# Trunk of four token mixers on one core: branch D's projections moved to the front, three gate paths moved into the seven-product stage

## The chip, the cores and the metric

One Trainium2 chip, one of its cores. The metric is the device time of one execution in microseconds (us); the times shown are of three runs. The engines are named as the profile names them: PE is TensorE (matmuls; PEld is its weight load), DVE is VectorE, ACT is ScalarE, POOL is GpSimd, SP is SyncE, which here only issues DMAs.

## What is computed

One layer over x of 512 tokens by 2048 columns, in float32. One projection of x is cut into the inputs of four mixers, their gate paths and four merge gates:

```
h = jnp.einsum('bsd,de->bse', x, w_in[l])
(a_in, a_gate, u, v, b_gate, q, k, vv, c_gate,
 d_in, d_gate, g_logits) = jnp.split(h, SPLIT_POINTS, axis=-1)

y_a = pool_mixer(a_in, pool_w[l], pool_scale[l]) * jax.nn.silu(a_gate)
y_b = spatial_gating(u, v, sgu_ln_g[l], sgu_ln_b[l], sgu_w[l], sgu_b[l]) * jax.nn.silu(b_gate)
y_c = sliding_window_attention(q, k, vv, attn_sinks[l], band_bias) * jax.nn.silu(c_gate)
y_d = conformer_conv(d_in, conv_w[l], conv_b[l], conv_ln_g[l], conv_ln_b[l]) * jax.nn.silu(d_gate)
...
merged = gates[:, :, 0] * jnp.einsum('bsc,cd->bsd', branches[0], w_branch[l, 0])
...
out = jnp.einsum('bsd,de->bse', merged, w_out[l])
x = layer_norm(ALPHA * x + out, ln_g[l], ln_b[l])
```

A pools over trailing windows of 2, 4, 8 and 16 tokens and multiplies by a small matrix per group. B normalises v and mixes it over tokens in chunks of 128. C is attention in a window of 128. D forms val * sigmoid(gate), convolves it over 31 tokens per channel (31 taps), normalises and applies swish. The gate paths a_gate, b_gate and d_gate (ag, bg and dg in the kernel) have 1024 columns each.

## The kernel before

Every large product is made of three matmuls (`mm3`, L137 to L139): both operands are split into a high part (hi, an ACT copy, L113) and a low part (lo, a DVE subtraction, L114), and hi x hi, lo x hi and hi x lo are summed in PSUM. Weights come in blocks of 512 KB; a block that is brought in and split is one *task* of PE.

There are two ways to make a projection. In a *projection tile* (`proj`), 128 columns of the weights are the stationary operand and all 512 tokens move past: 2 tasks of 24 matmuls, and the result has channels on the partitions. In the *seven-product stage* (`quad`) a set of 1024 columns is computed with seven products of half-size blocks in place of eight: p1, p5, m6, p3, m7, p2, p4, each 4 tasks of 12 matmuls, 336 in all. The results have tokens on the partitions and go to DRAM through ACT's queue (`spill`). The sums of weight blocks that the products need are made in place: after a block's hi and lo are taken, POOL issues a DMA that adds the next block onto the raw one (L288, tables `ADDS`, `TAKES`), and the next product splits it again. Tag `ra` carries the chain p1, p5, m6 (then p4), `rc` the pair p3, m7, `rd` p2. The sums of x blocks are made at the start (`first`, `xcalc`, `xsplit`). DVE adds the products up (L350); ACT copies the first (L354).

`run` (L168) walks a plan of tasks. The bringing in and splitting of a block runs two tasks ahead of its use (`AHEAD`), through four raw buffers and three of hi and lo. Ahead of each task `drain` issues some entries of a queue of side work (`bg`), which holds the taps of D's convolution (`conv`, L588 and L591): 248 of 128x512 on DVE. The framework's scheduler then sets the order within each engine; each engine runs its order strictly in turn.

The order before: 9 sets (v for branch B, then 8 for the merge gates); `back` brings back a block of x that a sum overwrote; D's val and gate tiles (16), with the taps on DVE behind them, and v's normalisation (`v_norm`) between them; branch B with u and bg in turn; branch A, with ag tiles behind each group's product (`pool_mix`, `group_mm`); the 8 dg tiles; attention; merge and output.

Of the kernel before, what the change touches and what calls it, by code (L numbers as in the profile page):

```python
# [17 lines left out]
P = 128  # L18
S = 512
# [18 lines left out]
QUADS = 9  # L38
# [14 lines left out]
def kernel(  # L53
# [52 lines left out]
    def bank():  # L106
        return pools["psum"].tile([P, S], F32, name="ps", tag="ps")
# [60 lines left out]
    def run():  # L168
# [3 lines left out]
        for prep, f in plan:  # L172
# [3 lines left out]
            while nxt < len(todo) and len(ready) <= AHEAD:  # L176
                ready.append(todo[nxt]())
                nxt += 1
# [7 lines left out]

    def proj(name, j, mid=()):
        i = SLOT[name, j]
        for c in range(2):
            def f(hi, lo, c=c):  # L190
                if c == 0:
                    box[name, j] = bank()
                for k in range(8):
                    kt = c * 8 + k
                    s_ = slice(k * P, (k + 1) * P)
                    mm3(box[name, j].rearrange("p (a b) -> p a b", a=2), hi[:, s_], lo[:, s_],
                        xmov(xH, kt), xmov(xL, kt), kt == 0, kt == KT - 1)
# [15 lines left out]
    def leave():  # L213
        opened.pop().__exit__(None, None, None)
# [10 lines left out]
    gD = dram.tile([len(ORDER), NB, P, D], F32, name="gD")  # L225
    yD = dram.tile([len(ORDER), WT, P, S], F32, name="yD")
# [8 lines left out]
    def enter_q():  # L235
        pools["pairs"] = enter("pairs", bass.MemoryType.PSUM)
        p = pools["quad"] = enter("quad")
        q["H"] = p.tile([P, len(SUMS), HT, 2 * P], F32R, name="sH")
        q["L"] = p.tile([P, len(SUMS), HT, 2 * P], F32R, name="sL")
        for n, a in enumerate(("x11", "x12", "s1", "x22")):  # L240
            q[a] = (xH[:, n], xL[:, n])
# [3 lines left out]
    def spin():  # L245
        w = pair(0)
        for _ in range(9):
            T.matmul(w[:, 0, :P], lhsT=ones, rhs=ones, start=True, stop=True)

    def pair(n):  # L250
        return pools["pairs"].tile([P, 2, S], F32, name=f"pr{n}", tag=f"pr{n}", bufs=1)

    def wide(name):
        return pools["quad"].tile([P, 2, S], F32, name="o", tag="o", bufs=4)

    def load_x(n, to):
# [7 lines left out]
    def xsplit(n, name, h):  # L264
# [873 lines left out]
```

## Time and profile before

| | |
|---|---|
| median of 3 runs | 2128.75 us (2128.35 to 2130.6) |
| profiled execution, its time | 2129.99 us |
| its span, first to last instruction | 2128.3 us |
| mean granted clock | 0.995 |
| PE busy | 2097.0 us (99%) |
| DVE busy | 1211.0 us (57%) |
| ACT busy | 751.0 us (35%) |
| POOL busy | 183.5 us (9%) |

An instruction's record is longer than its share of the engine where instructions overlap: a matmul is recorded with 0.39 us, but they start 0.23 us apart. Paces are therefore read from starts. The granted clock is the share of TensorE's full clock that it was given in a stretch.

### The profile page before, as it was taken

To read this page: it belongs to the slowest core of one execution; us is meant where nothing else is said; L and a number is where in the kernel's file an instruction comes from. 1 tells how busy PE (TensorE), PEld (TensorE's weight loads), DVE (VectorE), ACT (ScalarE), POOL (GpSimd) and SP (SyncE) were. 2 spreads that over 40 slices of the span, in tenths; PEclk is the share of its full clock that TensorE was granted. 3 is DMA by queue.
4 is the path that set the end of the run, shared out by engine and by line. 5 is a ranking of instruction groups with operands and counts; after the bars stand their busy time and mean duration, and the time that the engine had idled before them with its cause. 6 is when DMAs were issued, how large, how long until landed. Compare 5 with 4: busy or idle time off the path is not lost.

```text
span 2128.3 us, 23836 instructions
## 1 busy us (share of the span) xinstructions
PE 2097.0 (99%) x9436; PEld 1739.4 (82%) x9436; DVE 1211.0 (57%) x1467; ACT 751.0 (35%) x912; POOL 183.5 (9%) x241
## 2 busy tenths in 40 slices
PE   7999999999999999999999999999999999999998
PEld 5788888888888788888888888888888888888886
DVE  6555555555555699996353432366674445444346
ACT  5344444444444332222242222255562222222220
POOL 2021112112112100000000000000000000000002
PEclk8999999999999999999999999999999999999999
DMA  9998899899889622343323333423334454435332
GB/s 249 259 213 214 234 210 221 228 222 211 227 232 179 228 91 98 99 159 109 111 93 104 109 129 124 154 89 99 99 134 164 160 179 166 168 129 204 102 119 80
DMA packets 103552, 340.52 MB, mean 160 GB/s; under 512 B 10677, under 2 KB 15829, under 8 KB 102672
## 3 DMA queue, kind: packets, MB, share of 16 engines
q1 hardware_dynamic: 63232, 208.06, 29.9%
q0 software_dynamic: 29840, 111.40, 23.7%
q10 hardware_dynamic: 10368, 19.53, 2.4%
q8 instruction: 74, 1.21, 0.2%
q14 instruction: 38, 0.31, 0.0%
HBM read 307.47 MB, written 34.63 MB: 161 GB/s over the span
## 4 chain that ended last, share of the span: by engine, by line
PE 95%; DMA 2%; issue 1%; DVE 1%; POOL 0%; SPq 0%; ACT 0%; POOLq 0%; DVEq 0%; ACTq 0%
PE ps L137 21%; PE ps L138 21%; PE ps L139 21%; PE pr L138 10%; PE pr L139 10%; PE pr L137 10%; DMA rd<-in_xt 1%; PE ps L874 1%; PE ps L858 1%; DMA o<-in_xt 1%; DMA rc<-in_wq 0%; PE ps L810 0%; PE ps L809 0%; PE ps L467 0%; PE ps L554 0%
## 5 line engine op out<-in xcount | busy, mean ns | idle before, releaser
L114 DVE TENSOR_TENSOR lo<-ra,hi 128x1024 fp32r<-128x1024 f32 x387 | 471.0, 1217 | 718.1 <-ACT hi L113 694.1
L113 ACT CAST hi<-ra 128x1024 fp32r<-128x1024 f32 x387 | 405.9, 1049 | 1059.6 <-PE ps L138 447.8
L137 PE MATMUL ps<-xH,hi 128*128 128x512 f32 x1184 | 463.9, 392 | 2.1 <-DVE o L350 2.1
L139 PE MATMUL ps<-xH,lo 128*128 128x512 f32 x1184 | 461.4, 390 | 0.0
L138 PE MATMUL ps<-xL,hi 128*128 128x512 f32 x1184 | 461.4, 390 | 0.0
L137 PEld LDWEIGHTS ps<-xH,hi 128*128 128x128 f32 x1184 | 222.7, 188 | 48.9 <-issue 3.7
L139 PEld LDWEIGHTS ps<-xH,lo 128*128 128x128 f32 x1184 | 222.6, 188 | 46.8
L138 PEld LDWEIGHTS ps<-xL,hi 128*128 128x128 f32 x1184 | 222.8, 188 | 45.6 <-issue 0.5
L137 PE MATMUL pr<-hi,xH 128*128 128x512 f32 x576 | 226.4, 393 | 7.3 <-ACT hi L113 5.0
L138 PE MATMUL pr<-lo,xH 128*128 128x512 f32 x576 | 226.8, 394 | 5.3 <-DVE lo L114 5.3
L139 PE MATMUL pr<-hi,xL 128*128 128x512 f32 x576 | 226.2, 393 | 1.6 <-DVE xL L114 1.6
L137 PE MATMUL ps<-hi,xH 128*128 128x512 f32 x472 | 183.7, 389 | 0.0
L139 PE MATMUL ps<-hi,xL 128*128 128x512 f32 x472 | 183.6, 389 | 0.0
L138 PE MATMUL ps<-lo,xH 128*128 128x512 f32 x472 | 183.6, 389 | 0.0
L138 PE MATMUL pr<-lo,sH 128*128 128x512 f32 x432 | 168.4, 390 | 1.9 <-DVE lo L114 1.9
L137 PE MATMUL pr<-hi,sH 128*128 128x512 f32 x432 | 168.2, 389 | 1.5 <-ACT hi L113 1.5
L139 PE MATMUL pr<-hi,sL 128*128 128x512 f32 x432 | 168.1, 389 | 0.0
L591 DVE SCALAR_TENSOR_TENSOR conv<-glu,col,conv 128x512 f32<-128x512 f32 x240 | 164.0, 746 | 0.2
L288 POOL DMA_DIRECT2D ra<-in_wq x108 | 93.7, 868 | 481.7 <-DVE lo L114 409.0
L137 PEld LDWEIGHTS pr<-hi,xH 128*128 128x128 f32 x576 | 109.5, 190 | 30.8 <-ACT hi L113 5.3
L138 PEld LDWEIGHTS pr<-lo,xH 128*128 128x128 f32 x576 | 109.3, 190 | 29.5 <-DVE lo L114 6.7
L114 DVE TENSOR_TENSOR lo<-rc,hi 128x1024 fp32r<-128x1024 f32 x72 | 88.0, 1223 | 75.4 <-ACT hi L113 75.2
(198 smaller groups left out, 2328.6 us busy)
## 6 DMA issues: line engine op xcount, KB each, us to landing
ra<-in_wt SPq DMA_DIRECT2D x148, 512.0 KB, 3.4
ra<-in_wq POOLq DMA_DIRECT2D x108, 512.0 KB, 7.5
ra<-in_wb SPq DMA_DIRECT2D x64, 512.0 KB, 4.3
ra<-in_wq SPq DMA_DIRECT2D x36, 512.0 KB, 5.1
rc<-in_wq SPq DMA_DIRECT2D x36, 512.0 KB, 5.6
rd<-in_wq SPq DMA_DIRECT2D x36, 512.0 KB, 4.6
rc<-in_wq POOLq DMA_DIRECT2D x36, 512.0 KB, 7.2
gD<-o ACTq DMA_DIRECT2D x32, 512.0 KB, 6.7
```

What stands on the lines that cost most here:

```text
L113: A.copy(out=hi, in_=src)
L114: V.tensor_tensor(out=lo, in0=src, in1=hi.bitcast(F32), op=ALU.subtract)
L137: T.matmul(ps, lhsT=aH, rhs=bH, start=start, stop=False)
L138: T.matmul(ps, lhsT=aH, rhs=bL, start=False, stop=False)
L139: T.matmul(ps, lhsT=aL, rhs=bH, start=False, stop=stop)
L288: nc.gpsimd.dma_start(out=t, in_=block(n, ADDS[prod], c), accum_op=ALU.add)
L591: V.scalar_tensor_tensor(out=y, in0=src, scalar=cw(j, k), in1=y, op0=ALU.mult, op1=ALU.add)
L858: T.transpose(out=ps[:, o:o + P], in_=c["t", j, h][:, n, kb * P:(kb + 1) * P], identity=ident)
L874: T.matmul(o, lhsT=v[:, n - 1 + kb], rhs=p[:, ks], start=kb == blocks[0] and i == 0, stop=kb == 1 and i == 1)
```

## The change

D's val and gate tiles come first (`project_d`): eight at a time, first with the upper half of x's columns, then with the lower. The first two weight blocks and x come in interleaved pieces (`first_d`), and the x blocks and sums for the product stage are loaded and made between the tasks (`SIDE_WORK`). PSUM is then handed over (`to_pairs`). The stage has 12 sets: v, 8 merge gates, and bg, ag and dg, whose raw results go to a new DRAM buffer hD. The taps run beside the splits of the first sets, one queue entry per task in the plan. Tag `rd` is gone; p2's blocks go through `rc` and are fetched one product ahead. Then branch B runs u alone, three tiles ahead of the spatial unit, and branch A a alone. `turned` loads 512 KB of hD (two tiles) and turns it by 8 transposes on PE into PSUM, where the tile is used as before. The dg tiles are used in branch A, so D's end (`fin_d`) is there too. The diff, cut:

```diff
-QUADS = 9
+LATER = ("bg", "ag", "dg")
+QUADS = 9 + len(LATER)
...
 TILES = (
     [(n, j) for j in range(WT) for n in ("val", "gate")]
-    + [(n, j) for j in range(WT) for n in ("u", "bg")]
-    + [(n, j) for j in range(WT) for n in ("a", "ag")]
-    + [("dg", j) for j in range(WT)]
+    + [(n, j) for n in ("u", "a") for j in range(WT)]
     + [("k", 0), ("vv", 0)]
     + [(n, j) for j in range(WT) for n in ("q", "cg")]
...
+    def half_tile(name, j, c, hi, lo, ks=range(8)):
+        if c == 0 and ks[0] == 0:
+            box[name, j] = bank()
+        for k in ks:
+            kt = c * 8 + k
+            s_ = slice(k * P, (k + 1) * P)
+            mm3(box[name, j].rearrange("p (a b) -> p a b", a=2), hi[:, s_], lo[:, s_],
+                xmov(xH, kt), xmov(xL, kt), kt == 0, kt == KT - 1)
+
...
+    def turned(name, j):
+
+        def prep():
+            r = chunk("ra").rearrange("p (t c) -> p t c", t=NB)
+            nc.sync.dma_start(out=r, in_=hD[LATER.index(name), :, :, j * P:(j + 2) * P].rearrange("t p c -> p t c"))
+            return (r,)
+
+        def f(r):
+            for i in range(2):
+                ps = box[name, j + i] = bank()
+                for t in range(NB):
+                    T.transpose(out=ps[:, t * P:(t + 1) * P], in_=r[:, t, i * P:(i + 1) * P], identity=ident)
+        task(prep, f)
...
+    PLACE = {"11": "ra", "22": "rc", "21": "rc"}
...
+            if n == 0 and prod == "p5" and c == 0:
+                for h in range(2):
+                    xsplit(3, q["s1"], h)
             t = raw[n, TAKES[prod], c]
             made = split_new(t)
             if prod in ADDS:
                 nc.gpsimd.dma_start(out=t, in_=block(n, ADDS[prod], c), accum_op=ALU.add)
-            if n + 1 < QUADS and prod in ("m7", "p2", "p4"):
-                fetch(n + 1, TAKES[prod], c)
+            if prod == "m7":
+                fetch(n, "21", c)
+            if prod == "p2":
+                fetch(n + 1, "22", c)
+            if prod == "p4":
+                fetch(n + 1, "11", c)
+            if n == QUADS - 1 and prod == "p4":
+                back(c)
             return made
...
+    def back(c):
+
+        h = c % 2
+        if c < 2:
+            xs[2, h] = chunk("rc")
+            nc.sync.dma_start(out=xs[2, h], in_=xt[2, h])
+        else:
+            plain(2, h)
...
     def spill(n, t, th, ch):
-        if n > 0:
+        ts_, cs = slice(2 * th, 2 * th + 2), slice(ch * S, (ch + 1) * S)
+        if n == 0:
+            d = vD[ts_, :, cs]
+        elif n < 9:
             A.activation(out=t, in_=t, func=AF.Sigmoid)
-        cs = slice(ch * S, (ch + 1) * S)
-        if n == 0:
-            d = vD[2 * th:2 * th + 2, :, cs]
+            i, hq = divmod(n - 1, 2)
+            d = gD[i, ts_, :, hq * QW + ch * S:hq * QW + (ch + 1) * S]
         else:
-            i, hq = divmod(n - 1, 2)
-            d = gD[i, 2 * th:2 * th + 2, :, hq * QW + ch * S:hq * QW + (ch + 1) * S]
+            d = hD[n - 9, ts_, :, cs]
         nc.scalar.dma_start(out=d.rearrange("t p c -> p t c"), in_=t)
...
+    def first_d():
+
+        def prep():
+            pieces = [[load_x(n, h, 2) for n in (0, 2)] for h in range(2)]
+            w = []
+            for h in range(2):
+                for i in range(2):
+                    for p in pieces[h]:
+                        p[i]()
+                    if i == 0:
+                        w.append(load_raw(wt[h, 0]))
+            made = []
+            for h in range(2):
+                for i in range(2):
+                    for n in (0, 2):
+                        plain(n, h, slice(i * S, (i + 1) * S))
+                    if h == 0:
+                        made.extend(split_new(w[i]))
+            return made
+
+        def f(h0, l0, h1, l1):
+            for ks in (range(4), range(4, 8)):
+                half_tile("val", 0, 0, h0, l0, ks)
+                half_tile("gate", 0, 0, h1, l1, ks)
+        task(prep, f)
...
+    SIDE_WORK = (
+        [lambda n=n, h=h: bring(n, h) for n in (1, 3) for h in range(2)]
+        + [lambda n=n, h=h: plain(n, h) for n in (1, 3) for h in range(2)]
+        + [lambda: both(xcalc, 3, 2, 3, ALU.subtract), lambda: both(xcalc, 2, 0, 2, ALU.subtract),
+           lambda: both(xcalc, 0, 3, 0, ALU.subtract), lambda: both(xcalc, 1, 1, 0, ALU.add)]
+        + [lambda n=n, a=a, h=h: xsplit(n, q[a], h) for n, a in ((0, "S2"), (2, "s3"), (1, "s4")) for h in range(2)]
+    )
...
+    def project_d():
+        side = deque(SIDE_WORK)
+        first_d()
+        for g in range(2):
+            tiles = [(n, j) for j in range(4 * g, 4 * g + 4) for n in ("val", "gate")]
+            for c in range(2):
+                for n, j in tiles:
+                    if (c, j) == (0, 0):
+                        continue
+
+                    def prep(n=n, j=j, c=c):
+                        made = load_split(wt[SLOT[n, j], c])
+                        if side:
+                            side.popleft()()
+                        return made
+                    task(prep, lambda hi, lo, n=n, j=j, c=c: half_tile(n, j, c, hi, lo))
+                    if c == 1 and n == "gate":
+                        do(fin_glu, j)
+
...
+    def to_pairs():
+        leave()
+        pools["pairs"] = enter("pairs", bass.MemoryType.PSUM)
+
+    def from_pairs():
+        flush()
+        leave()
+        del pools["pairs"]
+        leave()
+        pools["psum"] = enter("psum", bass.MemoryType.PSUM)
+        pools["tmp"] = enter("tmp")
+
+    enter_d()
     enter_q()
+    pools["psum"] = enter("psum", bass.MemoryType.PSUM)
     spin()
-    begin()
-
...
+    nc.gpsimd.dma_start(out=col, in_=pcol)
+    nc.gpsimd.dma_start(out=sink, in_=sinks.partition_broadcast(P))
+    nc.gpsimd.dma_start(out=edge, in_=invc)
+    set_pace(1)
+    project_d()
+    do(conv_norm)
+    do(to_pairs)
     for n in range(QUADS):
         quad(n)
...
+    do(from_pairs)
...
     def branch_b():
+        do(enter_b)
+        proj("u", 0)
+        do(v_norm, 0)
+        proj("u", 1, [lambda: v_norm(1)])
+        do(v_norm, 2)
+        proj("u", 2, [lambda: v_norm(3)])
         for h in range(WT):
-            proj("u", h)
-            proj("bg", h)
+            if h % 2 == 0:
+                turned("bg", h)
             do(sgu, h)
             do(fin_b, h)
             if h == 0:
                 do(bias_rows)
             elif h < 5:
                 do(bias_table, h - 1)
+            if h + 3 < WT:
+                proj("u", h + 3)
...
             group_mm(g - 1)
-            for i in range(2):
-                proj("ag", 2 * (g - 1) + i)
-                do(fin_ag, 2 * (g - 1) + i)
-    do(leave)
-    do(flush)
-    for j in range(WT):
-        proj("dg", j)
-        do(fin_d, j)
-    do(leave)
-    do(enter_z)
+            turned("ag", 2 * g - 2)
+            for j in (2 * g - 2, 2 * g - 1):
+                do(fin_ag, j)
+            turned("dg", 2 * g - 2)
+            for j in (2 * g - 2, 2 * g - 1):
+                do(fin_d, j)
+
+    def leave_d():
+        leave()
+        leave()
+        leave(0)
+        pools["tmp"] = enter("tmp")
+        enter_z()
+    do(leave_d)
...
+    starts = [3072] + [base[f"g{i}"] + h * QW for i in range(len(ORDER)) for h in range(2)] + [base[n] for n in LATER]
```

What the built order shows at two places. First DVE's order. Before, in a set in the middle of the stage, with lo the splits of blocks (`ra`, `rc`) and L350 the sums of products:

```order
L114 TENSOR_TENSOR lo<-ra,hi 128x1024 x10
L114 TENSOR_TENSOR lo<-rc,hi 128x1024 x2
L350 TENSOR_TENSOR o<-pr_1368,o 128x1024
L114 TENSOR_TENSOR lo<-rc,hi 128x1024
L350 TENSOR_TENSOR o<-pr_1299,o 128x1024
L114 TENSOR_TENSOR lo<-rc,hi 128x1024 x3
L350 TENSOR_TENSOR o<-pr_1441,o 128x1024
L114 TENSOR_TENSOR lo<-rc,hi 128x1024 x2
```

After, from D's last tile (`glu` is its gated multiplication, L425) into the first products of set 0; L419 is a tap of the convolution:

```order
L115 TENSOR_TENSOR lo<-ra,hi 128x1024
L425 TENSOR_TENSOR glu<-ps,glu 128x512
L419 SCALAR_TENSOR_TENSOR conv<-glu,col,conv 128x512 x7
L115 TENSOR_TENSOR lo<-ra,hi 128x1024
L419 SCALAR_TENSOR_TENSOR conv<-glu,col,conv 128x512 x2
L115 TENSOR_TENSOR lo<-ra,hi 128x1024
L419 SCALAR_TENSOR_TENSOR conv<-glu,col,conv 128x512 x2
L115 TENSOR_TENSOR lo<-ra,hi 128x1024
L419 SCALAR_TENSOR_TENSOR conv<-glu,col,conv 128x512 x4
L115 TENSOR_TENSOR lo<-ra,hi 128x1024
L419 SCALAR_TENSOR_TENSOR conv<-glu,col,conv 128x512
L115 TENSOR_TENSOR lo<-ra,hi 128x1024
```

Between any two lo's there are now one to four taps, and seven behind the last gated multiplication.

The second place is the end of branch A on PE. Before, the product of the last group (mH and mL are the split pooling mix) stood inside projections (xH, xL):

```order
L138 MATMUL ps<-xL,hi 128x512
L139 MATMUL ps<-xH,lo 128x512
L137 MATMUL ps<-xH,hi 128x512
L138 MATMUL ps<-xL,hi 128x512
L139 MATMUL ps<-xH,lo 128x512
L137 MATMUL ps<-mH_7255,hi 128x512
L138 MATMUL ps<-mL_7256,hi 128x512
L139 MATMUL ps<-mH_7255,lo 128x512
L137 MATMUL ps<-mH_7255,hi 128x512
```

After, L215 being the transposes; mH_8390 is the mix of group 2 and mH_8392 that of group 3:

```order
L138 MATMUL ps<-mH_8390,hi 128x512
L139 MATMUL ps<-mL_8391,hi 128x512
L140 MATMUL ps<-mH_8390,lo 128x512
L215 MATMUL ps<-ident,ra 128x128 x16
L138 MATMUL ps<-mH_8392,hi 128x512 x2
L215 MATMUL ps<-ident,ra 128x128 x3
L139 MATMUL ps<-mL_8393,hi 128x512
L140 MATMUL ps<-mH_8392,lo 128x512
L138 MATMUL ps<-mH_8392,hi 128x512
L139 MATMUL ps<-mL_8393,hi 128x512
L140 MATMUL ps<-mH_8392,lo 128x512
```

The product of group 3 now follows that of group 2 with only transposes between them, where before the ag tiles 4 and 5, 96 matmuls, lay between the two.

## Rows read from the trace of the kernel before

**Rows 1.** Waits of PE over the span: us in total, times, longest

```profile
PE pr L138 <- DVE lo L114: 7.2, 6, 3.6
PE pr L137 <- ACT hi L113: 6.5, 2, 5.0
```

**Rows 2.** Busy by stage: PE, PEld, DVE, ACT, POOL (instructions), clock, DMA share, GB/s

```profile
0.00:40.00 40.00, 26.06 (x86) 20.24 (x87) 23.33 (x20) 21.23 (x22) 7.90 (x17) 0.83 0.95 282
130.00:207.00 77.00, 77.00 (x341) 63.79 (x340) 42.23 (x35) 35.61 (x35) 13.55 (x17) 1.00 0.93 219
800.00:900.00 100.00, 100.00 (x443) 82.81 (x442) 100.00 (x140) 21.61 (x24) 0.00 (x0) 1.00 0.30 95
```

**Rows 3.** Timeline of PE in a set: start us, recorded us, instruction

```profile
689.62 0.39 PE L139 MATMUL pr<-hi,sL 128*128 128x512 f32 x1
...
690.30 0.39 PE L139 MATMUL pr<-hi,sL 128*128 128x512 f32 x1
```

**Rows 4.** Timeline of PE in the merge stage, sixteen transposes and what follows

```profile
1882.00 1.91 PE L554 MATMUL ps<-ident,merged 128*128 128x128 f32 x16
1883.67 0.47 PE L137 MATMUL ps<-hi,yH 128*128 128x512 f32 x1
1883.98 0.39 PE L138 MATMUL ps<-lo,yH 128*128 128x512 f32 x1
```

**Rows 5.** The P copy's line: min/median/max ns, first and last start us

```profile
L354 ACT COPY o<-pr x9: 1002/1016/1016, 32.5 to 651.3; 128x1024 f32<-128x1024 f32 x9
```

**Rows 6.** Timeline of ACT and PE at the start

```profile
9.19 1.04 ACT L113 CAST hi<-ra 128x1024 fp32r<-128x1024 f32 x1 [2.43 <-DMA ra<-in_wq]
...
10.29 0.80 PE L137 MATMUL pr<-hi,xH 128*128 128x512 f32 x1 [5.02 <-ACT hi L113]
...
15.98 0.47 PE L139 MATMUL pr<-hi,xL 128*128 128x512 f32 x1
```

**Rows 7.** Timeline of PE where the sets end

```profile
718.67 0.47 PE L137 MATMUL ps<-xH,hi 128*128 128x512 f32 x1 [2.15 <-DVE o L350]
...
719.55 0.63 PE L137 MATMUL ps<-xH,hi 128*128 128x512 f32 x1
...
722.54 0.47 PE L138 MATMUL ps<-xL,hi 128*128 128x512 f32 x1
```

**Rows 8.** Timeline of DVE in D's projections: splits and taps

```profile
801.19 1.22 DVE L114 TENSOR_TENSOR lo<-ra,hi 128x1024 fp32r<-128x1024 f32 x1
802.33 4.73 DVE L591 SCALAR_TENSOR_TENSOR conv<-glu,col,conv 128x512 f32<-128x512 f32 x7
806.97 1.22 DVE L114 TENSOR_TENSOR lo<-ra,hi 128x1024 fp32r<-128x1024 f32 x1
```

**Rows 9.** DVE's product sums: busy, mean ns, idle before them and its releaser

```profile
L350 DVE TENSOR_TENSOR o<-pr,o 128x1024 f32<-128x1024 f32 x54 | 66.0, 1223 | 17.3 <-PE pr L139 17.3
```

**Rows 10.** An accumulate link (timeline), and such issues' landing (KB each, us)

```profile
425.72 1.05 ACT L113 CAST hi<-ra 128x1024 fp32r<-128x1024 f32 x1 [0.95 <-DMA ra<-in_wq]
...
428.43 0.86 POOL L288 DMA_DIRECT2D ra<-in_wq  x1 [1.14 <-DMA ra<-in_wq]
...
430.77 0.39 PE L137 MATMUL pr<-hi,xH 128*128 128x512 f32 x1
...
ra<-in_wq POOLq DMA_DIRECT2D x108, 512.0 KB, 7.5
```

**Rows 11.** The last step of v's normalisation: ns, first and last start us

```profile
L462 DVE TENSOR_TENSOR vn<-vn,b_bc x4: 1208/1220/1226, 741.9 to 759.3; 128x1024 f32<-128x1024 f32 x4
```

**Rows 12.** Pooling mix 3 (timeline): ACT's copy and DVE's last split

```profile
1215.48 0.58 ACT L688 COPY apad<-ps 128x512 f32<-128x512 f32 x1
...
1226.68 1.22 DVE L114 TENSOR_TENSOR mL<-mix,mH 128x1024 fp32r<-128x1024 f32 x1 [1.11 <-ACT mH L113]
```

**Rows 13.** Timeline: a POOL issue beside taps on DVE

```profile
971.31 0.54 POOL L204 DMA_DIRECT2D yD<-t  x1 [22.37 <-DVE t L479]
...
970.83 2.06 DVE L591 SCALAR_TENSOR_TENSOR conv<-glu,col,conv 128x512 f32<-128x512 f32 x3
```

More of the change, by code (lines that the diff above doesn't have):

```diff
@@ L175, in run @@
                 continue
-            while nxt < len(todo) and len(ready) <= AHEAD:
+            while nxt < len(todo) and sum(max(len(r) // 2, 1) for r in ready) <= AHEAD:
                 ready.append(todo[nxt]())
@@ L384, in quad, with enter_d @@
             prod(name, f)
-    def begin():
-        q["n"] = 0
-        def spare(h):
-            return wide("x").rearrange("p a b -> p (a b)")
-        load_x(0, lambda h: chunk("rd"))
-        for c in range(4):
-            fetch(0, "11", c)
-        load_x(2, spare)
-        load_x(3, spare)
-        for c in range(4):
-            fetch(0, "22", c)
-        load_x(1, lambda h: chunk("rd"))
+    dd = {}
+    def enter_d():
+        p = enter("poolD")
+        dd["x"] = p.tile([P, WT, PAD + S], F32, name="glu")
+        dd["y"] = p.tile([P, WT, S], F32, name="conv")
+        p.tile([P, 272], F32, name="pad")
+        G.memset(dd["x"][:, :, 0:PAD], 0.0)
@@ new lines, in fin_d, with set_pace @@
+    def fin_d(j):
+        s = half("s")
+        A.activation(out=s, in_=box["dg", j], func=AF.Silu)
+        t = half("t")
+        V.tensor_tensor(out=t, in0=dd["y"][:, j], in1=s, op=ALU.mult)
+        put_y(3, j, t)
+    def set_pace(n):
+        pace[0] = n
+    def first_d():
[21 more added lines that the diff above has]
+        task(prep, f)
@@ new lines, in bring, with both @@
+    def bring(n, h):
+        load_x(n, h)[0]()
+    def both(f, *a):
+        for h in range(2):
+            f(*a, h)
+    SIDE_WORK = (
[5 more added lines that the diff above has]
+    )
@@ L401, with spin @@
+    def spin():
+        w = bank()
+        for _ in range(9):
+            T.matmul(w[:, :P], lhsT=ones, rhs=ones, start=True, stop=True)
+    def to_pairs():
[9 more added lines that the diff above has]
+    enter_d()
     enter_q()
+    pools["psum"] = enter("psum", bass.MemoryType.PSUM)
@@ L646, in fin_d @@
-    def fin_d(j):
-        s = half("s")
-        A.activation(out=s, in_=box["dg", j], func=AF.Silu)
-        t = half("t")
-        V.tensor_tensor(out=t, in0=dd["y"][:, j], in1=s, op=ALU.mult)
-        put_y(3, j, t)
-    def set_pace(n):
-        pace[0] = n
-    def back():
-        for h in range(2):
-            t = chunk("ra")
-            nc.sync.dma_start(out=t, in_=xt[2, h])
-            hi, lo = (u[:, 2, 4 * h:4 * h + 4].rearrange("p k s -> p (k s)") for u in (xH, xL))
-            split(t, hi, lo)
@@ L664 @@
-    do(back)
-    do(enter_d)
-    do(enter_b)
-    do(set_pace, 5)
-    for j in range(WT):
-        proj("val", j)
-        proj("gate", j)
-        do(fin_glu, j)
-        if j < NB:
-            do(v_norm, j)
-    do(conv_norm)
-    branch_b()
     a = {}
```

216 lines of the change are left out of this document (86 added, 130 removed).

## Prediction

> **What bounds the kernel now.** I read the waits of TensorE (PE) first. The three that weigh are 7.2 us for a lo (the low half of a split block), 6.5 us for a hi (its high half) [rows 1], and 2.15 us at the change of stage [rows 7]. [...] The windows say where the loss lies: in the first 40 us PE is busy 26.06 us at a granted clock of 0.83, while a whole product set later (77 us) has PE busy 77.00 of 77 with VectorE (DVE) at 42.23; around 800 to 900 DVE is busy 100.00 of 100 and PE still 100.00 [rows 2]. So a full DVE does not by itself stop PE; but that was in projections, where half a tile lasts 5.44 us, not in product sets, where a task lasts 2.72.
>
> The unit of all that follows: L139 follows L139 after 0.68 us, with three matmuls in it, so one costs 0.2267 us [rows 3]. A task of 12 is 2.72 us, a product of four tasks 10.88, a set of seven products (336 matmuls) 76.16, a projection tile (48) 10.88.
>
> **The change, part by part.**
>
> 1. Matmuls. 24 tiles of gate paths (bg, ag, dg) leave: 24 x 48 = 1152. Three product sets come: 3 x 336 = 1008. That is 144 fewer, 144 x 0.2267 = **-32.6 us**. All of them lie on PE, at full pace, so I take this in full.
>
> 2. Transposes. Each of the 24 tiles is turned back in four 128x128 pieces: 96 more instructions on PE. The final stage has sixteen such between matmuls: they start at 1882.00, the next matmul at 1883.67, and that one is followed after 0.31 instead of 0.23: 1.75 us for 16, 0.109 each [rows 4]. 96 x 0.109 = **+10.5**. Behind those sixteen the matmuls go on at full pace, so I book nothing for the clock. [...]
>
> 3. The start. The P copy after the first product of a set runs 9 times, at 32.5 first and at 651.3 last [rows 5]. Eight sets and one product at full pace are 8 x 76.16 + 10.88 = 620.2, so 651.3 - 620.2 = 31.1 us have been lost by then. In the new order the first tiles need only x (pieces of 256 KB) and one weight chunk per 5.44 us, against one per 2.72 and three kinds of blocks before. The first hi of a weight starts at 9.19 behind 1 MB of x, PE at 10.29 [rows 6]; with 512 KB of x ahead of the weight I estimate PE's start at 8. The slow stretch after it, 10.29 to 15.98, holds 11 matmuls (2.49 us at full pace), so it is 3.2 us dearer [rows 6]; it stays. New loss 8 + 3.2 = 11.2, gain 31.1 - 11.2: **-19.9**. Bounds: -22 if PE starts at 7; -12 if x arrives as slowly as now (start at 10.3) and PE waits some 6 us more for later pieces of x.
>
> 4. From D's projections to the product sets. The PSUM pool changes hands, and the first product waits for the last gated-linear multiplication on DVE, which stands behind the third weight block's lo; the hi of that block needs the buffer that D's last task frees. So: hi 1.05, lo 1.14, multiplication 0.69, hand-overs: 3.1 us idle. The same kind of stop at the old change of stage is 2.15 us, and behind it, from 719.55 to 722.54, seven steps of about 0.43 [rows 7]: 7 x 0.2 = 1.4 us of slow clock, 1.6 with the uneven steps on either side. 3.1 + 1.6 = **+4.7** (2 to 6).
>
> 5. From the sets to branch B. The old stop there [rows 7] stays in kind: **0** (-2 to +1).
>
> 6. Convolution beside the sets. This is the step I know least. The order puts 65 taps (multiply-adds) of the convolution (and 4 cheaper first taps, counted alike) between the splits of set 0, 55 into set 1, 3 into set 2. One costs 0.663 (802.33 to 806.97 for seven), a lo 1.14 [rows 8]. Set 0 on DVE: 28 x 1.14 + 69 x 0.663 + 2 x 0.6 + 6 x 1.14 = 86 (the last two terms are gated multiplications and sums of products of 512 and 1024 columns); set 1: 28 x 1.14 + 55 x 0.663 + 7 x 1.14 = 76.4; PE's own 76.16 each, and about 8 us of set 0's share lies in D's tail. So DVE has no room left: 162.4 against 152.3 + 8. What it waits for products of PE (17.3 us in nine sets before [rows 9], so 3.8 in two) and what the accumulate chain loses is paid by PE. That chain: hi at 425.72, its POOL issue at 428.43, landing 7.5 later [rows 10]: 10.21 us of a period of 10.88, two links in a row (p1 to p5 to m6), one on the other chunks (p3 to m7). PE uses the block whose hi started at 425.72 only at 430.77: 5.05 minus hi and lo leaves 2.7 us in hand. One to three taps ahead of a lo are 0.7 to 2.0 us per link. Bounds: 0 if all of it fits into these 2.7 us, +20 if each of sets 0 and 1 is 8 to 10 us longer. I take **+8**: 2 + 4 from the DVE sum and about 1 for each set's chain.
>
> 7. Branch B without gate tiles ahead of it. The spatial unit needs the normalised v after u0, u1, u2 and one turned pair: 3 x 10.88 + 0.87 = 33.5 us after the stage starts. Before, the last step of the four starts at 759.31, 41.8 us after 718.67, drip-fed between the splits and taps of D [rows 11, 7]. Without the convolution on DVE it can be closer; **+2** (0 to 8).
>
> 8. End of branch A. Before, pooling mix 3 was covered by gate projections 4 and 5 (21.8 us). Now the last cover is one grouped product (12 matmuls, 2.72) and 16 + 3 transposes (2.1). The mix starts its copy at 1215.48 and its last lo ends at 1227.90: 12.4 us, 13.2 with the hand-over from PE [rows 12]. 13.2 - 4.8 = 8.4 us idle, then 1.6 of slow clock: **+10**. Bounds: 7 if the two weight splits that stand inside (2 x 1.14) come elsewhere, 12.
>
> DVE is free from set 3 on, and in branches B and A carries less than before; those hide themselves.
>
> Sum: -32.6 + 10.5 - 19.9 + 4.7 + 0 + 8 + 2 + 10 = -17.3. Against the profiled execution's own time of 2129.99 (its span is 2128.3) that is 2112.7; that execution is 1.24 us above the median of the runs shown, so I say **2111**.
>
> **Rivals.**
>
> (a) *Everything hides.* The 2.7 us in hand [rows 10] take the chain's delays, the mix comes out at +7, v_norm at 0, the start at -22: -32.6 + 10.5 - 22 + 4 + 7 = -33: 2096. For it: PE waited for nothing at DVE 100.00 [rows 2]. Against: a task in the sets is half as long.
>
> (b) *DVE sets the pace of sets 0 and 1.* DVE executes in order, so a sum that waits for a PE product holds the splits behind it. Step 6 at its upper end, +20 instead of +8: 2123.
>
> (c) *Slower than before: the accumulate chain breaks.* A lo that comes late makes POOL's issue late, that the landing, that the next hi on the same chunk. With L us added per link, a set loses (2L - 1.3 - 2.7) + (L - 0.7 - 2.7) = 3L - 7.4 (each link has 10.88 - 10.21 = 0.67 spare [rows 10]). Without step 6 the sum is -25.3, and some 2.6 sets are touched; the tie is at 9.7 per set, L = 5.7. With L = 8 it is 16.6 x 2.6 = 43: 2129.99 - 25.3 + 43 - 1.2 = 2146. For it: at most 0.67 spare per link; four taps in a row ahead of a lo are already 2.7. Against: it needs landings of 11 instead of 7.5 too, or POOL issues that DVE holds up. An issue of POOL at 971.31 took 0.54 in the middle of three taps that ran 970.83 to 972.89 [rows 13], so taps don't hold it. [...]
>
> [...]
>
> **How the numbers follow.** Forecast (2102 to 2120): 0.58. (a) 0.14, (b) 0.15, (c) 0.09, (d) 0.04. The range must leave out no more than 2 in 10: 2096 to 2127 leaves out (c), the lower half of (a) and a little of (b). A measurement tells a difference of about 0.2%, 4.3 us. Below 2124.5: all of the forecast and (a), two thirds of (b), half of (d), 0.83. Between 2124.5 and 2133: 0.08. Above: (c), 0.09.
>
> **What would show it.** Step 1 and 2: PE rows of L138 to L140 fewer by 144, 96 more transposes at 0.11 apart. Step 3: PE starts near 8, and has lost about 11 us by 40. Step 4: one wait of about 3 us before the first product of a set. Step 6: DVE near 100% from about 190 to 342; PE waits for hi or lo by some 8 us in sum there, and none from set 3 on; with (b) three times as much, with (c) waits of hi for the accumulate DMA in every product of sets 0 to 2. Step 8: one wait of about 8 us for mix 3's lo ahead of branch C. What would make it wrong: long waits in the first 40 us, or product sets whose period is over 80 us.

## The result, and the profile after

The changed kernel takes 2106.6 us (median of 4 runs, 2106.26 to 2108.14) against 2128.55 of the kernel before beside it: ratio 0.9898, 95% interval 0.9881 to 0.9915. That is 21.95 us less; the two profiled spans, on which the steps below are counted, differ by 23.8 (2104.5 against 2128.3). Forecast were 2111 us and a range of 2096 to 2127. In the experiments below the kernel before ran beside each batch again; its medians lay between 2128.04 and 2129.46, so a difference of 1 us between kernels of different batches says nothing by itself.

The page of the changed kernel: busy time and share of each engine, and the 40 slices for PE and DVE:

```profile
PE 2073.4 (99%) x9388; PEld 1722.9 (82%) x9388; DVE 1279.1 (61%) x1530; ACT 790.9 (38%) x954; POOL 227.3 (11%) x289
...
PE   8999999999999999999999999999999999999998
...
DVE  6799998555655555775566345466684445454346
```

DVE is now full from the third slice to the sixth (a slice is 52.6 us), where before it was full in the middle of D's projections. All waits of PE in the changed kernel (us in total, times, longest), to be held against [rows 1]:

```profile
PE ps L138 <- ACT mH L114: 8.9, 1, 8.9
PE ps L138 <- ACT hi L114: 5.0, 1, 5.0
PE pr L138 <- DVE glu L425: 4.2, 1, 4.2
PE ps L138 <- DVE o L366: 1.4, 1, 1.4
PE ps L548 <- POOL epst L233: 1.1, 1, 1.1
```

The waits of products for lo and hi of [rows 1] are gone. What is left are four single stops: the mix at the end of branch A (mH), the first weight block (hi), the hand-over of PSUM behind D (glu), and the end of the sets (L366, 1.4 instead of the 2.15 of [rows 7]). The fifth, 1.1 us for a constant (epst) at the very start, stood in the kernel before too.

Windows of the sets (PE, PEld, DVE, ACT, POOL busy; clock; DMA share; GB/s): set 0, set 1, and set 3, which carries no taps:

```profile
206.00:282.00 76.00, 76.00 (x337) 62.91 (x336) 75.98 (x92) 30.31 (x30) 13.60 (x16) 1.00 0.92 216
282.00:358.00 76.00, 76.00 (x337) 62.94 (x336) 75.72 (x90) 34.42 (x33) 13.85 (x16) 1.00 0.94 220
434.00:510.00 76.00, 76.00 (x337) 62.90 (x337) 42.22 (x35) 34.55 (x33) 13.88 (x16) 1.00 0.93 221
```

DVE is at 75.98 of 76 us, and PE at 76.00 of 76, as in a set with DVE at 42. The P copies (L370) say the same to the hundredth. ACT's timeline:

```profile
205.77 1.02 ACT L370 COPY o<-pr 128x1024 f32<-128x1024 f32 x1 [1.66 <-PE pr L140]
...
281.93 1.02 ACT L370 COPY o<-pr 128x1024 f32<-128x1024 f32 x1 [1.66 <-PE pr L140]
...
358.09 1.01 ACT L370 COPY o<-pr 128x1024 f32<-128x1024 f32 x1 [1.66 <-PE pr L140]
```

281.93 - 205.77 and 358.09 - 281.93 are both 76.16: the pace of PE alone.

The start, the hand-over from D to the sets, and the end of branch A, each from the timeline (ACT, PE and DVE rows):

```profile
9.20 1.04 ACT L114 CAST hi<-ra 128x1024 fp32r<-128x1024 f32 x1 [3.27 <-DMA ra<-in_wt]
...
10.30 0.80 PE L138 MATMUL ps<-xH,hi 128*128 128x512 f32 x1 [5.03 <-ACT hi L114]
...
187.43 0.39 PE L140 MATMUL ps<-xH,lo 128*128 128x512 f32 x1
192.05 0.80 PE L138 MATMUL pr<-hi,xH 128*128 128x512 f32 x1 [4.23 <-DVE glu L425]
...
197.34 0.45 PE L138 MATMUL pr<-hi,xH 128*128 128x512 f32 x1
...
186.18 4.07 DVE L419 SCALAR_TENSOR_TENSOR conv<-glu,col,conv 128x512 f32<-128x512 f32 x6
190.16 1.24 DVE L115 TENSOR_TENSOR lo<-ra,hi 128x1024 fp32r<-128x1024 f32 x1
191.29 0.70 DVE L425 TENSOR_TENSOR glu<-ps,glu 128x512 f32<-128x512 f32 x1
...
1309.64 1.91 PE L215 MATMUL ps<-ident,ra 128*128 128x128 f32 x16
1320.44 1.22 PE L138 MATMUL ps<-mH,hi 128*128 128x512 f32 x2 [8.89 <-ACT mH L114]
...
1317.28 0.69 DVE L478 TENSOR_TENSOR t<-conv,s 128x512 f32<-128x512 f32 x1 [2.06 <-DMA yD<-t]
...
1320.97 1.22 DVE L115 TENSOR_TENSOR mL<-mix,mH 128x1024 fp32r<-128x1024 f32 x1
```

PE starts at 10.30, as before [rows 6]. Between the last matmul of D and the first of set 0 lie 4.2 us, and then twelve matmuls at a granted clock of 0.50: 192.05 to 197.34 is 5.29 us instead of 2.72. The lo that the last gated multiplication stands behind started at 190.16, behind six taps. At the end of branch A, PE stands idle for 9 us between the sixteen transposes and the first matmul of mix 3; a sum of D's output (L478) that waits 2.06 us for an earlier store to land stands in the middle of the mix's chain.

### The profile page after: what moved, and what is told of

Same layout as the page of the kernel before. It is cut to its first block, busy times and chain, and to the rows that moved or that the text cites. A ratio compares the mean times of both kernels' runs of the same rounds, so it can differ in the third digit from the quotient of the medians.

```text
span 2104.5 us, 24063 instructions
## 1 busy us (share of the span) xinstructions
PE 2073.4 (99%) x9388; PEld 1722.9 (82%) x9388; DVE 1279.1 (61%) x1530; ACT 790.9 (38%) x954; POOL 227.3 (11%) x289
## 4 chain that ended last, share of the span: by engine, by line
PE 90%; DVE 6%; issue 3%; DMA 1%; ACT 0%; POOL 0%; SPq 0%; POOLq 0%; DVEq 0%
PE pr L138 15%; PE pr L139 15%; PE ps L138 15%; PE pr L140 15%; PE ps L139 14%; PE ps L140 14%; DVE conv L419 4%; DVE lo L115 1%; PE ps L941 1%; PE ps L925 1%; PE ps L877 0%; PE ps L876 0%; DMA ra<-in_wt 0%; PE ps L622 0%; PE ps L719 0%
## 5 line engine op out<-in xcount | busy, mean ns | idle before, releaser
L115 DVE TENSOR_TENSOR lo<-ra,hi 128x1024 fp32r<-128x1024 f32 (+1 forms) x387 | 470.8, 1217 | 608.1 <-ACT hi L114 587.0
L114 ACT CAST hi<-ra 128x1024 fp32r<-128x1024 f32 (+1 forms) x387 | 405.9, 1049 | 924.4 <-PE ps L140 345.7
L138 PE MATMUL ps<-xH,hi 128*128 128x512 f32 x800 | 314.5, 393 | 6.4 <-ACT hi L114 5.0
L140 PE MATMUL ps<-xH,lo 128*128 128x512 f32 x800 | 312.6, 391 | 0.0
L139 PE MATMUL ps<-xL,hi 128*128 128x512 f32 x800 | 312.4, 391 | 0.0
L138 PE MATMUL pr<-hi,xH 128*128 128x512 f32 x768 | 300.4, 391 | 4.2 <-DVE glu L425 4.2
L140 PE MATMUL pr<-hi,xL 128*128 128x512 f32 x768 | 299.7, 390 | 0.0
L139 PE MATMUL pr<-lo,xH 128*128 128x512 f32 x768 | 299.7, 390 | 0.0
L115 DVE TENSOR_TENSOR lo<-rc,hi 128x1024 fp32r<-128x1024 f32 x144 | 176.0, 1222 | 104.1 <-ACT hi L114 104.1
L114 ACT CAST hi<-rc 128x1024 fp32r<-128x1024 f32 x144 | 151.6, 1052 | 202.8 <-PE pr L140 195.7
```

The costliest lines, as they stand in the source:

```text
L114: A.copy(out=hi, in_=src)
L115: V.tensor_tensor(out=lo, in0=src, in1=hi.bitcast(F32), op=ALU.subtract)
L138: T.matmul(ps, lhsT=aH, rhs=bH, start=start, stop=False)
L139: T.matmul(ps, lhsT=aH, rhs=bL, start=False, stop=False)
L140: T.matmul(ps, lhsT=aL, rhs=bH, start=False, stop=stop)
```

## Experiments

### The two halves of the change apart

D first, without the gate paths in the sets:

```diff
-LATER = ("bg", "ag", "dg")
+LATER = ()
...
-            if h % 2 == 0:
-                turned("bg", h)
+            proj("bg", h)
...
-            turned("ag", 2 * g - 2)
...
+                proj("ag", j)
```

> The changed kernel with the three gate paths bg, ag and dg back as projection tiles (9 sets instead of 12, no turning), D's projections still first: one half of the change alone. Theory: the halves add up. D first is worth the start (31.1 us lost before, 13.9 in the trace of the changed kernel, -17.2), less the hand-over from D to the sets (4.4 us idle and 2.6 of slow clock, +7.0) and the shorter stop behind the sets (-2.3): -12.5, so about 2116, and PE waits for no mix at the end of branch A, since the ag tiles cover it again. Rival: the start gains only because the sets come later with everything loaded, and the convolution beside the sets costs what the gate sets hide elsewhere: then this kernel is near before, 2124 or more.

Measured: 2115.68 us, ratio 0.9944 (0.9929 to 0.9959), 12.4 us less than before. The expected size, and no wait for a mix.

The gate paths in the sets, D where it was (in the kernel before: `QUADS = 12`, raw results to DRAM, `turned` in place of bg, ag and dg, and the dg pairs in a row behind branch A):

```diff
-QUADS = 9
+LATER = ("bg", "ag", "dg")
+QUADS = 9 + len(LATER)
...
-    for j in range(WT):
-        proj("dg", j)
-        do(fin_d, j)
+    for j in range(0, WT, 2):
+        turned("dg", j)
+        do(fin_d, j)
+        do(fin_d, j + 1)
```

> The kernel before with the gate paths bg, ag and dg moved into the sets (12 sets, raw results to DRAM, turned later), D's projections behind the sets as before: the other half alone. Theory: 144 matmuls less (-32.6) and 96 transposes more (+10.5), and the pooling mix at the end of branch A loses its cover (+10 to +12): -10 to -12, so 2117 to 2119, with the start's 31 us still lost. Rival: the gain of the gates lives off D being first (the convolution then no longer fits behind D and u alone, and DVE makes PE wait in branches B and A): 2122 to 2130, with PE waits on DVE between the end of the sets and branch C.

Measured: 2126.94 us, ratio 0.9996 (0.9986 to 1.0005): no gain. The time is the rival's, the cause is not: behind the stop at the end of the sets PE has no wait on DVE before branch C. Windows around the end of branch A in this kernel:

```profile
1320.00:1330.00 10.00, 3.84 (x16) 2.51 (x14) 7.23 (x9) 2.13 (x3) 1.08 (x2) 0.78 0.30 105
1330.00:1340.00 10.00, 7.19 (x45) 6.32 (x44) 1.41 (x2) 2.28 (x4) 1.08 (x2) 0.84 0.55 156
1340.00:1350.00 10.00, 7.28 (x20) 5.10 (x20) 6.18 (x7) 5.19 (x7) 2.18 (x4) 0.52 0.91 343
```

and the longest waits of PE in this stretch:

```profile
PE ps L136 <- ACT mH L112: 6.1, 1, 6.1
...
PE ps L213 <- DMA ra<-hD: 2.8, 1, 2.8
...
PE ps L136 <- ACT hi L112: 2.7, 1, 2.7
```

From 1320 to 1350 us PE has 48 transposes, 12 matmuls of the mix and some 15 of branch C to do, about 11.4 us at full pace (48 x 0.109 + 27 x 0.2267). So some 18 of the 22 us that the matmuls gain are lost in one place, for want of anything to cover the mix and the loads of the turned tiles: 6.1, 2.8 and 2.7 us of waits, the rest at granted clocks down to 0.52 (1340 to 1350). In the changed kernel the dg pairs lie in branch A between projections, and only the mix is left uncovered. So the halves do not add up as kernels (12.4 and 1.1 us apart, 21.95 together): what the second is worth depends on where its short work lies.

### What a full DVE costs in the sets

Four kernels change only the taps: how many there are, and how they are queued. Their convolution is another one than D's.

```diff
-            for k in range(CK):
+            for k in range(1):
```

> The changed kernel with 30 of the 31 taps of the convolution left out (only the first tap is done): what the full DVE costs in sets 0 and 1. Theory: nothing there; only the hand-over from D to the sets gets shorter, because its split no longer stands behind six taps: -1.5 to -2.5, 2104 to 2105. Rival (step 6 of the prediction): the taps do cost PE some 8 us in the sets, in small delays that no wait shows: 2098 to 2099.

Measured: 2104.29 us (2103.03 to 2105.59), 2.3 below the changed kernel. Its wait for glu is 2.8 instead of 4.2 us, with 1.6 us of slow matmuls behind it instead of 2.6. Its sets have the period 76.16 too, but for the first, 77.99, which takes the two small matmuls of the convolution's mean and variance that the changed kernel has in sets 8 and 9 (77.07 each). So the taps cost nothing in the sets, and about 2.4 us at the hand-over.

```diff
-                    bg.append(lambda jj=jj, k=k: conv(jj, k))
+                    bg.append(lambda jj=jj, k=k: [conv(jj, k), conv(jj, k) if k else None])
```

> The changed kernel with every tap but the first done twice (so D's convolution is another one): 159 us more of DVE work, which has to lie in the sets. Theory: a full DVE does not stop PE as long as the order gives each split its place, so DVE is full for two to three more sets and PE waits under 3 us more: 2106 to 2109. Rival: DVE executes in order and has no slack at 100%, so each further full set loses 3 to 8 us: 2115 to 2140, with PE waits for lo in the sets.

Measured: 2106.87 us, as the changed kernel. DVE is full through set 5, and PE waits 1.1 us for lo.

```diff
+                    bg.append(lambda jj=jj, k=k: [conv(jj, k) for _ in range(3 if k else 1)])
```

> The changed kernel with every tap but the first done three times (another convolution): 318 us more of DVE work than in the changed kernel. DVE's whole demand over D and the 12 sets is then about 1030 us of the 1090 that these take. Theory: DVE is full for nine or ten sets and PE still waits only some tenths of a us per set, 2107 to 2111. Rival: small delays grow with each full set (the doubled taps showed 1.1 us of waits for lo), 2115 or more.

Measured: 2199.36 us, ratio 1.033 (1.0313 to 1.0347), 93 us above the changed kernel. My theory fell here. Waits of PE in this kernel (us, times, longest):

```profile
PE pr L138 <- ACT hi L114: 26.4, 23, 3.0
PE pr L139 <- DVE lo L115: 26.2, 32, 2.0
```

and a window from the sets, with the columns of the windows above:

```profile
700.00:850.00 150.00, 134.90 (x547) 105.39 (x546) 150.00 (x189) 54.22 (x52) 27.77 (x32) 0.95 0.83 179
```

PE is busy 134.90 of 150 us, at a granted clock of 0.95, while DVE is at 150.00 of 150. Counting what DVE executed from the first split of a set to the first of the next, and pricing it with 0.663 per tap, 0.63 per sum of 512 columns and 1.135 per split or wide sum (28 and 7 of them, 39.7 us), gives DVE's demand as an estimate, beside the periods measured between P copies:

```
set                          0..2        3      4      5      6      7      8
thrice: taps                 52 to 67    77     84     84     80     84     23
thrice: DVE demand, us       74 to 84    90.8   95.4   95.4   92.8   95.4   68.8
thrice: period, us           76.2        93.7   95.4   93.6   94.1   95.4   78.0
twice: taps                  54 to 66    55     55     57     25     0      0
twice: period, us            76.2, 76.9  76.2   77.2   76.2   76.2   76.2   77.1
```

The copy lies one product into its set, so a period takes a part of the next set's demand; part of set 0's taps lie in D's tail. With three taps to an entry of the side queue and one entry per task, 28 x 3 = 84 taps were forced into a set in which 55 fit; the excess of the demand over 76.16, summed over sets 3 to 7, is 89 us, and the kernel lost 93. (Where the taps are all done, sets 8 and 9 carry the two small matmuls of the convolution's mean and variance: 77.1.)

The last of the four does the same work with one tap to an entry:

```diff
+                    for _ in range(3 if k else 1):
+                        bg.append(lambda jj=jj, k=k: conv(jj, k))
```

> The same work as with the taps done three times (another convolution than the reference's), but each tap is its own entry of the side queue and not three to an entry. The built order then has 54 to 55 taps in each of sets 1 to 9, where three to an entry gave 78 to 84 in sets 3 to 7 (DVE demand by trace costs 76.2 us per set against 91 to 95). Theory: what counts is the demand in each set against PE's 76.16, not the sum: PE pays the excess and nothing below it, so this kernel is at 2107 to 2110 with set periods of 76.2 throughout. Rival: a DVE that is full for ten sets drifts late by its small waits, and PE pays for the sum of the work: 2120 or more.

Measured: 2126.98 us, ratio 0.9989 (0.9979 to 0.9999). The time is the rival's (2120 or more), some 20 us above the changed kernel and 17 above the theory; the cause is not the rival's. The periods are 76.16 to 77.2 in all ten full sets, nearly as the theory said, and the loss lies in one place behind them. PE's waits in this kernel:

```profile
PE pr L464 <- DVE glu L436: 15.3, 1, 15.3
...
PE pr L139 <- DVE lo L115: 1.0, 4, 0.4
```

L464 is the variance's matmul. The taps ended so late that the convolution's normalisation was no longer hidden by the sets: 15.3 us in one wait, and between 1060 and 1140 PE is busy 63.97 of 80 us at a granted clock of 0.87 (in the changed kernel 78.59 at 1.00). In the sets, PE waited 1.0 us for lo. So it is the demand within each set that counts, and a chain that must end before the stage does needs its own room. Long runs of taps ahead of one split are not the cause: in sets 1 and 2 of both kernels up to five stand in a row, and the periods are 76.16 to 76.21.

### The four stops one by one

One PSUM pool from the start; val j and gate j share a pair buffer:

```diff
+            if name == "val":
+                box["pair", j] = pair()
+            if name in ("val", "gate"):
+                box[name, j] = box["pair", j][:, name == "gate"]
...
-    pools["psum"] = enter("psum", bass.MemoryType.PSUM)
+    pools["pairs"] = enter("pairs", bass.MemoryType.PSUM)
...
-    do(to_pairs)
```

> The changed kernel with one PSUM pool from the start: val j and gate j of D take the two halves of one pair buffer, so the first product of the sets waits for a pair that was free long ago and not for the last gated multiplication. Theory: the hand-over (4.2 us idle in the trace of the changed kernel, then 12 matmuls in 5.3 instead of 2.7 us) goes as a whole: -6.5 to -7, 2099.5 to 2100. Rival: the stop gave DVE 7 us in which PE asked for nothing, and DVE is at 75.98 of 76 us in set 0; without it PE waits for lo in sets 0 and 1 instead, 3 to 6 us: 2102 to 2106.

Measured: 2099.94 us, ratio 0.9862 (0.9848 to 0.9877), 6.7 below the changed kernel. PE's waits here hold no glu, and for lo:

```profile
PE pr L139 <- DVE lo L115: 0.4, 1, 0.4
```

So the stop was not what gave DVE its room: without it set 0 keeps its 76.16, and set 1 takes 76.84.

The k and vv projections ahead of the last group's product:

```diff
+        if g == len(WINDOWS):
+            proj("k", 0)
+            proj("vv", 0)
         if g:
             group_mm(g - 1)
...
-    proj("k", 0)
...
-    proj("vv", 0)
```

> The changed kernel with the k and vv projections (96 matmuls, 21.8 us) ahead of the last group's product at the end of branch A: the pooling mix is covered again. Theory: the wait for mH (8.9 us) and the slow clock behind it (about 1.5) go: -10 to -11, 2096. Rival: the wait only moves, since PSUM buffers held by k and vv make the turned tiles or attention wait: 2100 to 2106.

Measured: 2094.48 us, ratio 0.984 (0.9824 to 0.9857), 12.1 below the changed kernel, and no PE wait on mH at all. In the changed kernel's trace the stop accounts for 11.0 of it: 9.05 us from the end of the transposes to 1320.44, and 1.95 of slow matmuls and transposes behind. The rest lies elsewhere: the slow stretches at the start and behind the hand-over lose 2.5 and 1.7 us in this kernel's trace, and 3.2 and 2.6 in the changed kernel's.

The three small loads behind the first x and weight blocks, on SP's queue:

```diff
+        + [load_small]
...
-    nc.gpsimd.dma_start(out=col, in_=pcol)
-    nc.gpsimd.dma_start(out=sink, in_=sinks.partition_broadcast(P))
-    nc.gpsimd.dma_start(out=edge, in_=invc)
```

> The changed kernel with the three small loads (140, 8 and 32 KB, issued by POOL at 1.70 to 2.98 us) moved behind the first x and weight blocks on SP's queue. Between 6.3 and 8.5 us the DMA rate falls to some 80 GB/s in both kernels, at the time when these small packets are under way. Theory: they hold up the first weight block; without them it lands at about 7.5 instead of 9.2, PE starts at 8 to 9, and the time is 1 to 2 us less: 2104.6 to 2105.6. Rival: the hole has another cause, PE starts at 10.3 again, 2106.6.

Measured: 2104.5 us, ratio 0.9886 (0.9871 to 0.99). The start, ACT's first weight split and PE's first matmul:

```profile
7.80 1.04 ACT L114 CAST hi<-ra 128x1024 fp32r<-128x1024 f32 x1 [2.11 <-DMA ra<-in_wt]
...
8.89 0.79 PE L138 MATMUL ps<-xH,hi 128*128 128x512 f32 x1 [3.62 <-ACT hi L114]
```

PE starts 1.4 us earlier than the changed kernel's 10.30. One trace proves little here, though: in the kernels of this study whose first loads are those of the changed kernel, PE's first matmul was seen at 10.30, 10.80, 10.69, 10.69, 10.03, 7.61, 10.56 and 8.25. The medians differ by 2.1 us, within their intervals. The pair at the end of this section tells more.

All three:

> The changed kernel with the three edits together (one PSUM pool, k and vv ahead of the last group product, small loads late). Theory: they add up, -17.5 to -20: 2087 to 2089. Rival: without the stop at the hand-over DVE is late in sets 0 and 1 and gives back 3 to 6 us: 2091 to 2095.

Measured: 2087.37 us, ratio 0.9804 (0.9789 to 0.9819), 19.2 below the changed kernel; apart they gave 6.7 + 12.1 + 2.1 = 20.9. And with the first two weight blocks in halves:

```diff
+                    cs = slice(h * S, (h + 1) * S)
+                    nc.sync.dma_start(out=w[i][0][:, cs], in_=wt[i, 0][:, cs])
```

> The three edits together, and the first two weight blocks in halves of 256 KB, so that 768 KB instead of 1 MB have to land ahead of PE's first matmul. Theory: PE starts at 7 instead of 8.5, and the time falls by 1 to 1.5 us to about 2086. Rival: the start is bound by the bytes that D's first group needs in sum (3 MB by 13 us), so PE waits later for what it gained, 2087 to 2088.

Measured: **2084.5 us**, ratio 0.9789 (0.9774 to 0.9803), the fastest of all here. PE's first two matmuls:

```profile
6.43 0.50 PE L138 MATMUL pr<-xH,hi 128*128 128x512 f32 x1 [1.16 <-ACT hi L114]
6.76 0.40 PE L139 MATMUL pr<-xL,hi 128*128 128x512 f32 x1
```

They start at 6.43, and the second follows after 0.33, where [rows 6] and the changed kernel have a slow stretch with 0.43 and more from matmul to matmul. The gain is more than I had expected (2.9 us instead of 1 to 1.5), because I had counted the earlier start alone. By the first P copy (196.93 with whole blocks, 193.59 here) 3.3 us are gained: 2.1 from the start (8.49 to 6.43), and 1.3 because the slow stretch of 3.3 us has given way to short waits that lose 2.0, the longest of them 0.80 for a split of x. PE had stood idle for 1.16 us before its first matmul here, and for 2.3 to 6.0 in every other kernel, all of which have the slow stretch. The last kernel is this one with the small loads back on POOL's queue at the start:

> The fastest kernel so far (one PSUM pool, k and vv early, small loads late, first weight blocks in halves) with the small loads back at the start on POOL's queue. PE's start has meanwhile been seen between 7.61 and 10.80 us in kernels whose first loads are the same, so the single look at 8.89 without the small loads proves little. Theory: the small loads do hold up the first blocks; PE starts 1 to 2 us later than 6.43 and the time is 1 to 2.5 us above 2084.5. Rival: they don't, the start scatters by itself; the time is within 0.7 us of 2084.5.

Measured: 2086.91 us (2086.2 to 2087.64, 5 runs) against 2083.54 to 2085.45 with the small loads late, 2.4 us more. ACT's first weight split and PE's first matmul:

```profile
8.80 0.62 ACT L114 CAST hi<-ra 128x512 fp32r<-128x512 f32 x1 [2.92 <-DMA ra<-in_wt]
...
9.47 0.80 PE L138 MATMUL pr<-xH,hi 128*128 128x512 f32 x1 [4.20 <-ACT hi L114]
```

The kernel before ran at 2128.43 and 2128.55 beside the two. Their first P copies lie 2.53 us apart (196.12 and 193.59); by the end of the two traces 1.2 are left. So the small loads do hold up the first weight block, though not in every execution. The windows from 7 to 8 us say when: of the nine traces with the small loads at the start, seven show 89 to 165 GB/s there and PE's first matmul at 9.47 to 10.80, and two (D first, taps spread) show 271 and 249 and a start at 7.61 and 8.25. The three traces with the small loads late show 258 to 340 and starts at 6.43 to 8.89. Why the other two have no hole is not shown. What the half blocks are worth without the late loads was not measured.

## Why the prediction was right, step by step

The time fell in the range and the sign was right, but the sum was 6.5 us too small in the spans (-17.3 against -23.8), and single steps were off by more, in both directions. By the table, steps 2, 5, 6 and 7 were forecast 12.8 us too dear, and steps 3, 4 and 8 5.9 us too cheap; that these cancelled in part, so that the time came out 4.4 us from the forecast, is luck.

| step | forecast | measured | from |
|---|---|---|---|
| 1 matmuls | -32.6 | -32.6 | 48 fewer on each of the three lines |
| 2 transposes | +10.5 | +10 | 96 of them (L215); 13 in a row take 1.34 |
| 3 start | -19.9 | -17.3 | P copy 205.77 |
| 4 hand-over | +4.7 | +7.0 | 4.4 idle (192.05 - 187.43 - 0.23), 2.6 slow |
| 5 end of the sets | 0 | -2.3 | 1.41 idle, no slow stretch |
| 6 taps beside the sets | +8 | 0 | period 76.16 |
| 7 normalised v | +2 | 0 | no such wait |
| 8 end of branch A | +10 | +11.0 | 9.05 idle, 1.95 slow |

The column measured sums to -24.2, against -23.8 of the spans.

**Steps 1 and 2** came out as counted. Rival (d), a clock that falls behind turned groups, had no row of before to show it, and did not happen. PE's timeline behind one of them:

```profile
1257.14 1.91 PE L215 MATMUL ps<-ident,ra 128*128 128x128 f32 x16
1258.80 0.47 PE L138 MATMUL ps<-xH,hi 128*128 128x512 f32 x1
1259.12 0.39 PE L139 MATMUL ps<-xL,hi 128*128 128x512 f32 x1
1259.34 0.39 PE L140 MATMUL ps<-xH,lo 128*128 128x512 f32 x1
```

The matmuls go on 0.32 and then 0.22 us apart, and from 1143 to 1310, with six of the eight groups in it, the granted clock is 1.00. Of all the turned groups only the one behind the 9 us of idle time has slow matmuls.

**Step 3.** The first P copy starts at 205.77; D's 16 tiles and one product take 174.1 + 10.88 = 185.0 at full pace, so 20.8 us are lost, of which 7.0 belong to step 4. The 13.8 left exceed the 11.2 forecast by 2.3 for PE's start (10.30, not 8) and by 0.2 from the product's last matmul to its copy, which the 31.1 had in it and the 11.2 had not; the slow stretch was 3.2, as forecast. The term that was off is the landing of the first weight block. I scaled it by the bytes ahead of it, but the three small loads are under way at the same time, and the landing scatters: PE's start lay between 7.61 and 10.80 in kernels with the same first loads. The 8 was at the early end of this. Without the small loads and with half blocks PE started at 6.43.

**Step 4.** I counted hi, lo and multiplication one after another from the freeing of the buffer. In the trace DVE executes in the built order, and six taps (186.18 to 190.16) stood ahead of that lo. They stand in the built order one row above those that I read. That is 1.3 us of idle time, and the slow stretch was twelve matmuls and not eight.

**Step 5.** The same kind of stop was 1.41 instead of 2.15 us, and the matmuls behind it start 0.30, 0.24 and then 0.23 apart, with no slow stretch:

```profile
1112.01 0.47 PE L138 MATMUL ps<-xH,hi 128*128 128x512 f32 x1 [1.41 <-DVE o L366]
1112.31 0.40 PE L139 MATMUL ps<-xL,hi 128*128 128x512 f32 x1
1112.55 0.40 PE L140 MATMUL ps<-xH,lo 128*128 128x512 f32 x1
```

**Step 6** is the term that was wrong, +8 for 0. The demand of 162.4 us against a room of 160.3 was right to 2 us; the rest was not a cost. I added what DVE waited for products in sets where it was half empty [rows 9]; a full DVE comes to the sums later, and the products are there. The sums in sets 0 and 1, then in sets 3 and 4 (busy, mean ns, idle and releaser):

```profile
L366 DVE TENSOR_TENSOR o<-pr,o 128x1024 f32<-128x1024 f32 x12 | 14.6, 1219 | 0.0
...
L366 DVE TENSOR_TENSOR o<-pr,o 128x1024 f32<-128x1024 f32 x12 | 14.7, 1223 | 4.1 <-PE pr L140 4.1
```

And I charged the accumulate chain for delays that fit into its 2.7 us in hand, though none to five taps stood ahead of a split in set 1 and up to seven at the start of set 0, more than the one to three that I counted with. The chain was never late. ACT's longest waits in sets 0 and 1 (us, times, longest):

```profile
ACT hi L114 <- PE pr L140: 76.3, 49, 1.7
ACT hi L114 <- DVE lo L115: 5.0, 3, 1.7
```

and POOL's accumulate issues there and in sets 3 and 4 (busy, mean ns, idle and releaser):

```profile
L311 POOL DMA_DIRECT2D ra<-in_wq x24 | 20.7, 865 | 110.4 <-DVE lo L115 110.4
...
L311 POOL DMA_DIRECT2D ra<-in_wq x24 | 20.8, 866 | 110.0 <-DVE lo L115 91.4 <-DMA ra<-in_wq 18.6
```

No hi waits for an accumulate DMA in the sets where DVE is full, and an issue takes 865 ns beside the taps and 866 without. That settles rival (c): taps (multiply-adds on two arrays in float32) do not hold up POOL's issues here. Rival (b) did not happen either, but the kernel with three taps to an entry shows that it is real: where a set's demand on DVE was 91 to 95 us, PE paid the whole excess over 76.16. The changed kernel stands right at that edge, at 56 taps in set 1 by the executed order. One entry per task would put 28 into a set; the framework's scheduler filled the sets beyond that, and in the kernels with more taps it stopped at 52 to 58 wherever the queue did not force more.

**Step 7.** PE waited for no normalised v. With DVE free of taps there, the last of the four steps started 31.7 us after the stage did (1143.69 against 1112.01) and ended at 1144.92, 0.7 us before the matmuls that read v began (1145.64). So it was close. The 41.8 us of before run to the end of that step, not to its start, which lies 40.6 us behind 718.67 [rows 11, 7]; they were a drip-feed and no need.

**Step 8** had the right place and nearly the right size; the wait ended with mH, not with the last lo. From the copy (1307.12) to the end of the last lo (1322.19) the chain took 15.1 us instead of 12.4; part of it is the 2.06 us in which a sum of D's output waited for a buffer.

Rival (a), everything hides, was right for steps 6 and 7, but not for the start and the end of branch A.

## What to carry to other kernels

When work moves in between an engine's due pieces, compare its demand with the period stretch by stretch, piece by piece of the built order: below the period it was free here, even at 75.98 of 76 us, and above it the other engine paid the whole excess (89 us by the estimate, 93 lost). Then see that the last of the work, and what waits for it, still ends before the stage does. Long work can also be the cover of something else: before a projection is replaced by a cheaper way, list which chains it hides, and put independent work in its place (k and vv here, some 11 us). And look for the places where a whole pool of buffers changes hands: giving the buffers out in the next stage's shape took 6.7 us away without any new work.

## What the runs showed of the hardware that was not expected

Three small loads of 140, 8 and 32 KB, issued by POOL at 1.7 to 3 us, go with a hole in the DMA transfers (89 to 165 GB/s between 7 and 8 us in seven of nine traces): in the fastest kernel 2.4 us of the time hang on them, and PE's first matmul moved from 6.43 to 9.47 with them. And the stops are dearer than they look where the clock falls behind them: 4.4 us idle at the hand-over cost 7.0 (granted clock 0.50 over the next 5.29 us), 9.05 us at the end of branch A 11.0 (0.70 over the next 5.56 us), while 1.41 us at the end of the sets (1.00 over the next 3.99 us) and 1.16 us before the first matmul of the fastest kernel had no slow stretch behind them.
